# Gates of a delta-rule layer projected one round sooner and held in the buffers of y

## The chip, the cores and the metric

The kernel runs on one core of one Trainium2 chip. The core has five engines with a queue of instructions each: TensorE (PE, the matrix multiplier; its weight loads are listed as PEld), VectorE (DVE), ScalarE (ACT), GpSimd (POOL) and SyncE (SP, which here only starts transfers). The metric is device microseconds of one execution of the whole program. Three runs of the kernel before gave 2085.65, 2086.14 and 2088.14 us, median 2086.14.

## The reference

Two residual layers over 512 tokens of width 2048, float32. Layer 0 is gated differential attention, and this change doesn't touch it. Layer 1 is gated RWKV-7 time mixing, with 32 heads of 64 channels:

```
x = x + rwkv7_mixer(rms_norm(x), ...)

def rwkv7_mixer(h, ...):
    p = h @ w_in
    p = p + (token_shift(p) - p) * mu              # mix with the token before
    r, k, v, g, dw, da = split(p)
    decay, a = f(tanh(dw) @ decay_up), sigmoid(a0 + da @ iclr_up)
    kk = normalised(k * k_k);  k = k * (1 + (a - 1) * k_a)
    # S <- S*decay + (S @ -kk) (kk*a)^T + v k^T ;  y = S @ r     for each token, per head
    y = wkv7_scan(r, decay, k, v, -kk, kk * a)
    y = group_norm(y) * gn_w + gn_b + sum(r * k * r_k) * v
    return (y * silu(g)) @ w_out
```

## The kernel before

**Precision.** A float32 product is made of three TensorE products of operands split into a high and a low part (`mm3`, L118): 128 rows of weights, 512 tokens wide. Each weight tile is loaded by SP, its high part is cast by ACT (L109) and its low part subtracted by DVE (L110).

**Rounds.** Layer 1 (`layer1`, L1674) works on pairs of heads, 128 channels at a time, in sixteen rounds j = 0 to 15. A projection (`proj(i, j)`, `unit_chan`) of r, k, v or g for one pair is 16 k-steps of three matmuls, 48 in all; its result lies in one of two banks of PSUM until ACT and DVE mix it with the token before (`shift_mix`, L1173, lines L1177 and L1178). A round j issues in order: the values of pair j (`stage_v`), the keys of pair j + 1 (`begin`), from round 2 on the gate of pair j - 2 (`gate`, then `gated`), and the receptance of pair j + 1 (`receptances`). Round 1 has thus three projections, rounds 2 to 14 four, round 15 two. The gates of pairs 14 and 15 are projected after the last round, and then the output projection follows.

**The chunked scan.** The delta rule runs over eight chunks of 64 tokens. For pair j, `gram` makes the chunks' Gram matrices behind a matmul of the values' projection; `t_solve` (L1438 on) inverts their triangular 32 x 32 blocks in 31 dependent steps of two DVE operations (L1459, L1462), and turns the result (L1467, L1472); `t_first` and `t_second` (L1493, L1508) put the inverse of the 64 x 64 blocks together with small matmuls; `mask_gram` masks on POOL (L1411, L1413). One round later `scan_pair` (L1574 on) goes through the chunks: per chunk a matmul with the state (L1585), copies by ACT (L1588), a matmul with the inverse (L1598), copies (L1600), and a matmul with the keys (L1607) whose result DVE adds to the state (L1611; L1614 in the first chunk). Then the outputs are normalised, `finish_y` (L1669, L1671) transposes them, scales them and adds them to y, which `stage_v` has begun (L1524), and `gated` multiplies y into the gate (L1552) and stores the product in `yd2` (L1555), from where the output projection reads it.

**What sets the order.** Each matmul of a projection counts as a tick (`tick`). The scan is a list of steps that are issued so many ticks apart: `chain(g, j - 1, pair, delay, gap, gap_s, others)` waits `delay` ticks, then `gap` ticks after the first and the second matmul of a chunk and `gap_s` after the third; `others` are pieces hung on a chunk's end (`finish_y` on chunk 5). The solve is issued likewise, every three or four ticks (in the last round two or three), after a first pause of ten ticks or six. Pieces can also be hung on the n-th matmul of a projection ("behind"): the Gram matrices on 18 of the values (12 in round 1); in the receptance of round j - 1, `t_first` on 12, `mask_gram` on 27, `t_second` on 33 for j from 3 on, and on 24, 45 and 42 for j = 2. `t_first` issues at once whatever steps of the solve are left. From this, from priorities and from modelled durations a planner writes a fixed order for each engine's queue before the program runs; on the chip an engine takes its queue strictly in that order, waiting where an operand isn't ready.

**Buffers.** y has four buffers (`tag="y"`), taken in turn. The gate is mixed in the one buffer that the values have too (`tag="v"`), is multiplied there and stored from there.

Of the kernel before, what the change touches and what calls it, by code (L numbers as in the profile page):

```python
# [13 lines left out]
F32 = mybir.dt.float32  # L14
# [9 lines left out]
P = 128  # L24
D = 2048
T = 512
# [501 lines left out]
class Seven:  # L528
# [70 lines left out]
    def behind(self, raw, h, i):  # L599

        if h + 1 < NH:
            landed = self.g.nc.gpsimd.tensor_copy(self.mark[:], raw[:, 0, 0:1])
            with self.g.tc.issue_after(landed.ins):
                self.prime(h + 1, True, GROUPS[i : i + 1])
        return raw
# [566 lines left out]
@urgent  # L1172
def shift_mix(g, ps, rows, mu, omu, tag, bufs=2):  # L1173

    nc, w = g.nc, g.work
    o_ = w.tile([P, T], F32, name="mix" + tag, tag=tag, bufs=bufs)
    nc.scalar.activation(o_[:rows, :], ps[:rows, :], AF.Copy, scale=omu)  # L1177
    nc.vector.scalar_tensor_tensor(o_[:rows, 1:], ps[:rows, 0 : T - 1], mu, o_[:rows, 1:], ALU.mult, ALU.add)  # L1178
    return o_
# [77 lines left out]
LAG = 2  # L1257
# [11 lines left out]
def sum_channels(g, out, ones, x):  # L1269

    h, l = x
    g.nc.tensor.matmul(out, ones, h[:], start=True, stop=False)
    g.nc.tensor.matmul(out, ones, l[:], start=False, stop=True)
# [164 lines left out]
def t_solve(g, j, p):  # L1438


    nc, w = g.nc, g.work
    NQ = HALF // NG
    yield 3
    LT = g.low.tile([P, HALF, HALF], F32, name="LT", tag="LT", bufs=1)
    lt = nc.vector.transpose(LT[:].rearrange("p (r c) t -> p t r c", r=NG),
                        p.LP[:].rearrange("p c t -> p t c")[:, :, None, :].to_broadcast([P, HALF, NG, NC_]))
    Tm = w.tile([P, NQ, HALF], F32, name="Tm", tag="Tm", bufs=1)
    tmp = w.tile([P, NQ * HALF], F32, name="tmpl", tag="tmpl", bufs=1)
    nc.gpsimd.tensor_copy(Tm[:], g.unit[:])
    n2 = p.n2  # L1450
    behind(g, lt)
    with g.tc.issue_after(lt.ins):
        nc.vector.tensor_scalar(n2[:], n2[:], 1e-24, None, ALU.max)
        nc.vector.reciprocal(n2[:], n2[:])
    yield 10 if j >= LAG else 6
    for i in range(HALF - 1):
        n, s = HALF - 1 - i, i // NG + 1
        tt = tmp[:, : n * s].rearrange("p (a b) -> p a b", a=s)
        st = nc.vector.scalar_tensor_tensor(tt, LT[:, i : i + 1, i + 1 :].to_broadcast([P, s, n]), n2[:, i : i + 1],  # L1459
                                       Tm[:, 0:s, i : i + 1].to_broadcast([P, s, n]), ALU.mult, ALU.mult)  # L1460
        behind(g, st)
        nc.vector.tensor_add(Tm[:, 0:s, i + 1 :], Tm[:, 0:s, i + 1 :], tt)  # L1462
        yield (3 if j + 1 < D // P else 2) + i % 2
    nc.vector.tensor_mul(Tm[:], Tm[:], n2[:, None, :].to_broadcast([P, NQ, HALF]))
    p.T1 = w.tile([P, NC_, HALF], F32, name="T1", tag="T1", bufs=1)
    yield 9
    tt = nc.vector.transpose(p.T1[:].rearrange("p c (q r) -> p q r c", r=NG),  # L1467
                        Tm[:].rearrange("p q (r c) -> p q r c", r=NG))
    p.W = w.tile([P, NC_, HALF], F32, name="W", tag="Tm", bufs=1)
    behind(g, tt)  # L1470
    yield 4
    tt = nc.vector.transpose(p.W[:], p.T1[:])  # L1472
    behind(g, tt)
    for h in range(2):
        for half in range(2):
            o = half * HALF
            q = slice(h * C + o, h * C + o + HALF)
            nc.gpsimd.tensor_copy(g.TT[j % 2][q, :, h, o : o + HALF], p.W[q])
# [38 lines left out]
def stage_v(g, j, p, vps):  # L1517
    nc, w = g.nc, g.work
    col = lambda n: g.prm[n][:, j : j + 1]
    ps = g.ps.tile([P, 512], F32, name="pt", tag="pd", bufs=1)  # L1520
    sum_channels(g, ps[:], g.ones[:], split_act(g, p.rf[:], w, "x"))
    v = shift_mix(g, vps, P, *mus(g, 2, j), "v", 1)
    p.y = w.tile([P, T], F32, name="y", tag="y", bufs=4)
    nc.vector.tensor_mul(p.y[:], ps[:], v[:])  # L1524
    nc.scalar.activation(p.y[:], p.y[:], AF.Identity, bias=col("hgb"))
    p.v = v
# [15 lines left out]
def gate(g, j, gps, tag="v"):  # L1542
    nc, w = g.nc, g.work
    gt = shift_mix(g, gps, P, *mus(g, 3, j), tag, 1)
    th = w.tile([P, T], F32, name="thg", tag="thg", bufs=1)
    nc.scalar.activation(th[:], gt[:], AF.Tanh, scale=0.5)
    nc.vector.scalar_tensor_tensor(gt[:], th[:], 1.0, gt[:], ALU.add, ALU.mult)
    return gt


def gated(g, j, p, gt, last=False):
    g.nc.vector.tensor_mul(gt[:], gt[:], p.y[:])  # L1552
    if last:
        return
    g.nc.scalar.dma_start(out=g.yd2[j * P : (j + 1) * P, :], in_=gt[:])  # L1555
# [118 lines left out]
def layer1(g, aps):  # L1674
    nc, tc = g.nc, g.tc
    with ExitStack() as cx:
        g.lc = cx.enter_context(tc.tile_pool(name="lc1", bufs=1))
        g.work = cx.enter_context(tc.tile_pool(name="work1", bufs=2))
        rwkv_masks(g)
        w = g.work  # L1680
        pairs = []

        def proj(i, j, **k):
            return unit_chan(g, aps["rw_w_in"][i, j], P, **k)[0]
# [26 lines left out]
        for j in range(D // P):  # L1711
            p = pairs[j]
            if j:
                others = [(1, lambda p=p: turn_keys(g, p, 0)), (2, lambda p=p: turn_keys(g, p, 4)),
                          (4, lambda p=p: turn_values(g, p))]
                if j > 1:
                    others.append((5, lambda i=j - 2: finish_y(g, i, pairs[i])))
                full = LAG <= j < D // P - 1
                gaps = (7, 8) if full else (5, 6) if j > 1 else (4, 5)
                chain(g, j - 1, pairs[j - 1], 3 if j > 1 else 22, *gaps, others)  # L1720
            stage2(g, j, r, p)

            def behind(m, j=j, p=p):
                if j > 1:
                    pairs[j - 2].chain.finish(g)
                with tc.issue_after(m.ins):
                    gram(g, j, p)
                p.solve = Solve(g, t_solve(g, j, p))
            hooks = [(12 if 0 < j < LAG else 18, behind)]
            if j + 1 == D // P:  # L1730
                hooks.append((39, lambda m, p=p: [mask_gram(g, p, h, m) for h in range(2)]))
            stage_v(g, j, p, proj(2, j, behind=hooks))
            turns = ()
            if j == 0:
                turns = ((9, lambda m: turn_keys(g, p, 0)), (15, lambda m: turn_keys(g, p, 4)),
                         (27, lambda m: turn_values(g, p)))
            if j + 1 < D // P:
                begin(j + 1, turns)
            if j >= LAG:
                gated(g, j - LAG, pairs[j - LAG], gate(g, j - LAG, proj(3, j - LAG)))  # L1740
            if j + 1 < D // P:
                r = receptances(j + 1)
        chain(g, j, p, 3, 4, 5, whole=True)
        gps = proj(3, j - 1)
# [132 lines left out]
```

## Time and profile before

| | us |
|---|---|
| median of three runs | 2086.14 |
| profiled execution, its own time | 2087.84 |
| its span, first to last instruction | 2086.1 |
| layer 1's rounds, from the first receptance's end to the last one's | 977.5 to 1843.3 |
| round 1, round 2 | 53.2, 63.5 |
| each of rounds 3 to 13 | 59.1 to 59.2 |
| round 14 | 59.0 |

The profile is one execution; times are counted from its first instruction. PE is 99% busy, DVE 80%, ACT 60%, POOL 19%. A busy PE isn't a PE at its peak, since matmuls overlap in the array and their ends are modelled: what matters is the time from one matmul's start to the next, and the waits. Lines of groups read: line, engine, operation, out<-in, shapes, count | busy us, mean ns | idle time of the engine before them and what ended it. In a list of waits stand the total, the count and the longest. A round is counted here from the evacuation of one receptance (`mixr`, L1177 on ACT) to that of the next.

### The profile page before, as it was taken

What the parts mean: (1) busy time and instruction counts of PE and PEld (TensorE: products, weight loads), DVE (VectorE), ACT (ScalarE), POOL (GpSimd) and SP (SyncE); (2) the same over time, 40 slices, a digit from 0 to 9 for tenths busy, and PEclk for the clock granted to TensorE, in tenths of its full rate; (3) what the DMA queues carried; (4) which work ended last, traced back from release to release, by engine and by line L of the source; (5) the groups of instructions that cost most, each with busy time, mean ns of one, the idle gap of its engine ahead of it and who ended that gap; (6) DMA issues with size and microseconds to landing.
All of it is one profiled execution on the core that took longest, in us unless ns stands there. A gap on an engine that the chain in (4) does not pass through costs nothing.

```text
span 2086.1 us, 35354 instructions
## 1 busy us (share of the span) xinstructions
PE 2067.0 (99%) x12008; PEld 1708.6 (82%) x12008; DVE 1664.8 (80%) x4353; ACT 1250.9 (60%) x3005; POOL 406.2 (19%) x716
## 2 busy tenths in 40 slices
PE   9999999999999999999999999999999999999999
PEld 8888888888888888888778888888888888877887
DVE  5978778787877886576888888888888888887745
ACT  5766665666666664455666666666666666655333
POOL 0111011111111000101233332233333332342001
PEclk9999999999999999999999999999999999999999
DMA  6576777777777766742212222222222222235665
GB/s 200 146 181 178 182 187 190 181 193 180 190 175 192 182 222 196 169 118 93 79 64 79 80 78 69 82 79 82 76 79 79 79 79 74 89 126 166 204 163 120
DMA packets 101782, 280.71 MB, mean 135 GB/s; under 512 B 12545, under 2 KB 29073, under 8 KB 101601
## 3 DMA queue, kind: packets, MB, share of 16 engines
q1 hardware_dynamic: 68064, 198.90, 29.1%
q0 software_dynamic: 19104, 63.55, 16.4%
q10 hardware_dynamic: 14432, 16.01, 2.2%
q8 instruction: 94, 1.54, 0.3%
q14 instruction: 88, 0.71, 0.1%
HBM read 262.42 MB, written 15.99 MB: 133 GB/s over the span
## 4 chain that ended last, share of the span: by engine, by line
PE 92%; DVE 5%; ACT 2%; issue 1%; DMA 0%; POOL 0%; ACTq 0%; DVEq 0%; POOLq 0%
PE pp L118 70%; PE pt L118 6%; PE gp L1366 1%; PE sc L118 1%; PE sm L1585 1%; PE o L118 1%; PE sm L1607 1%; PE lora L118 1%; PE sm L1598 1%; PE z L118 1%; PE Y L1631 1%; DVE wl L110 1%; PE pt L359 1%; PE pt L1426 1%; PE px L1493 0%
## 5 line engine op out<-in xcount | busy, mean ns | idle before, releaser
L118 PE MATMUL pp<-hH,wh 128*128 128x512 f32 x1024 | 416.9, 407 | 0.0
L118 PE MATMUL pp<-hL,wh 128*128 128x512 f32 x1024 | 412.5, 403 | 0.0
L118 PE MATMUL pp<-hH,wl 128*128 128x512 f32 x1024 | 412.0, 402 | 0.0
L109 ACT CAST wh<-wraw 128x512 fp32r<-128x512 f32 (+1 forms) x412 | 253.8, 617 | 200.5 <-PE pp L118 103.5
L110 DVE TENSOR_TENSOR wl<-wraw,wh 128x512 fp32r<-128x512 f32 (+1 forms) x412 | 286.3, 696 | 102.6 <-ACT wh L109 98.7
L118 PE MATMUL pp<-wh,hH 128*128 128x512 f32 x932 | 366.5, 393 | 0.0
L118 PE MATMUL pp<-wh,hL 128*128 128x512 f32 x932 | 366.5, 393 | 0.0
L118 PE MATMUL pp<-wl,hH 128*128 128x512 f32 x932 | 364.4, 391 | 0.0
L118 PEld LDWEIGHTS pp<-hH,wh 128*128 128x128 f32 x1024 | 192.9, 188 | 37.6 <-issue 1.8
L118 PEld LDWEIGHTS pp<-hH,wl 128*128 128x128 f32 x1024 | 193.2, 189 | 32.8
L118 PEld LDWEIGHTS pp<-hL,wh 128*128 128x128 f32 x1024 | 193.3, 189 | 31.2
L118 PEld LDWEIGHTS pp<-wh,hL 128*128 128x128 f32 x932 | 175.1, 188 | 35.9
L118 PEld LDWEIGHTS pp<-wl,hH 128*128 128x128 f32 x932 | 175.2, 188 | 35.3 <-DVE wl L620 0.2
L118 PEld LDWEIGHTS pp<-wh,hH 128*128 128x128 f32 x932 | 175.3, 188 | 34.2
L620 DVE TENSOR_TENSOR wl<-wraw,wh 128x512 fp32r<-128x512 f32 x224 | 152.4, 688 | 60.0 <-ACT wh L619 59.4
L619 ACT CAST wh<-wraw 128x512 fp32r<-128x512 f32 x224 | 138.2, 620 | 93.8 <-PE pp L118 66.6
L1593 POOL COPY SA<-VS 64x64 f32<-64x64 f32 x224 | 75.1, 335 | 522.8 <-DVE VS L1611 466.4
L118 PE MATMUL pp<-wh,S 128*128 128x512 f32 x504 | 162.1, 395 | 0.0
L1459 DVE SCALAR_TENSOR_TENSOR tmpl<-LT,n,Tm 128x60 f32<-128x60 f32 (+24 forms) x496 | 135.6, 273 | 13.3
L582 POOL DMA_DIRECT2D T<-in_da_w_in_dram x63 | 53.7, 857 | 327.8 <-DVE wl L620 314.5
L1462 DVE TENSOR_TENSOR Tm<-Tm,tmpl 128x60 f32<-128x60 f32 (+24 forms) x496 | 106.2, 214 | 13.6
L619 ACT CAST wh<-T 128x512 fp32r<-128x512 f32 x126 | 77.8, 618 | 52.3 <-PE pp L118 52.2
(373 smaller groups left out, 3973.2 us busy)
## 6 DMA issues: line engine op xcount, KB each, us to landing
wraw<-in_rw_w_in_dram SPq DMA_DIRECT2D x128, 512.0 KB, 3.4
wraw<-in_da_w_in_dram SPq DMA_DIRECT2D x127, 512.0 KB, 4.3
T<-in_da_w_in_dram POOLq DMA_DIRECT2D x63, 512.0 KB, 6.1
wraw<-in_da_w_out_dram SPq DMA_DIRECT2D x26, 512.0 KB, 4.4
wraw<-in_rw_w_out_dram SPq DMA_DIRECT2D x26, 512.0 KB, 3.9
T<-in_da_w_in_dram SPq DMA_DIRECT2D x21, 512.0 KB, 4.3
wraw<-in_da_w_in_dram POOLq DMA_DIRECT2D x21, 512.0 KB, 6.9
yr<-yd SPq DMA_DIRECT2D x20, 256.0 KB, 3.1
```

Of the source, the lines that this page charges most:

```text
L109: nc.scalar.copy(hi[:], raw[:, k : k + n])
L110: g.split = nc.vector.tensor_sub(lo[:], raw[:, k : k + n], hi[:].bitcast(F32)).ins
L118: m = nc.tensor.matmul(out, a, b, start=s, stop=e, skip_group_check=skip)
L359: nc.tensor.transpose(pt[:, c * P : (c + 1) * P], t1s[t][:, c * P : (c + 1) * P], g.ident[:])
L582: self.g.nc.gpsimd.dma_start(out=raw, in_=src, accum_op=ALU.add)
L619: g.nc.scalar.copy(hi[:], raw[:, k])
L620: g.nc.vector.tensor_sub(lo[:], raw[:, k], hi[:].bitcast(F32))
L1366: m = nc.tensor.matmul(gp[h][:, i * P : (i + 1) * P], BK[r_, c0 + i, :, :], p.AR[r_, c0 + i, :, :], start=True, stop=True)
L1426: nc.tensor.transpose(ps[:, i * P : (i + 1) * P], p.BK[:, c0 + i].rearrange("p s t -> p (s t)"), g.ident[:])
L1459: st = nc.vector.scalar_tensor_tensor(tt, LT[:, i : i + 1, i + 1 :].to_broadcast([P, s, n]), n2[:, i : i + 1], Tm[:, 0:s, i : i + 1].to_br ...
L1462: nc.vector.tensor_add(Tm[:, 0:s, i + 1 :], Tm[:, 0:s, i + 1 :], tt)
L1593: nc.gpsimd.tensor_copy(p.SA[r_, c - 1, :], VS[r_, c, h, :])
```

## The change

One gate projection moves from round 14 to round 1. Rounds 1 to 13 project the gate of pair j - 1 and hold it, unmultiplied, for a round; round 14 projects none; round 15 projects that of pair 13, as before. The gate of pair j - 2, held since the round before, is multiplied with y and stored at matmul 36 of the next gate's projection (in round 14 after the keys' projection, in round 15 after the gate).

y and the held gates share four buffers that are allocated once and handed round in a list (`g.ys`). `shift_mix` with no tag takes the next of the list; after the product, the buffer of the gate goes back to the list first and the one of y behind it, so that in rounds 2 to 13 the new gate is mixed in the buffer whose product has just been sent to be stored.

The scan's gaps change with the work of the rounds: (6, 7) in round 1 instead of (4, 5), (5, 6) in rounds 14 and 15 (round 14 had (7, 8)), (7, 8) in the others. The solve's first pause is ten ticks from round 1 on (it was six in rounds 0 and 1). The matmuls on which `t_first`, `mask_gram` and `t_second` hang stay as they are.

```diff
@@ shift_mix
-    o_ = w.tile([P, T], F32, name="mix" + tag, tag=tag, bufs=bufs)
+    o_ = w.tile([P, T], F32, name="mix" + tag, tag=tag, bufs=bufs) if tag else g.ys.pop(0)
@@ t_solve
-    yield 10 if j >= LAG else 6
+    yield 10 if j else 6
@@ stage_v
-    p.y = w.tile([P, T], F32, name="y", tag="y", bufs=4)
+    p.y = g.ys.pop(0)
@@ layer1
+        g.ys = [w.tile([P, T], F32, name="y", tag="y", bufs=4) for _ in range(4)]
...
-                full = LAG <= j < D // P - 1
-                gaps = (7, 8) if full else (5, 6) if j > 1 else (4, 5)
+                gaps = (6, 7) if j == 1 else (7, 8) if j < D // P - 2 else (5, 6)
                 chain(g, j - 1, pairs[j - 1], 3 if j > 1 else 22, *gaps, others)
...
                 begin(j + 1, turns)
-            if j >= LAG:
-                gated(g, j - LAG, pairs[j - LAG], gate(g, j - LAG, proj(3, j - LAG)))
+            def finished(m, i=j - LAG):
+                with tc.issue_after(m.ins):
+                    gated(g, i, pairs[i], held)
+                g.ys.extend((held, pairs[i].y))
+
+            if j == D // P - 2:
+                finished(g.m)
+            elif j:
+                last = j == D // P - 1
+                gps = proj(3, j - 1 - last, behind=[(36, finished)] if j >= LAG and not last else ())
+                held = gate(g, j - 1 - last, gps, None)
+                if last:
+                    finished(g.m)
             if j + 1 < D // P:
                 r = receptances(j + 1)
```

## The prediction

> **What bounds the kernel now.** I read the page first, then the second layer cut at the ends of its rounds, then what TensorE (PE) waits for there. From the page:
>
> ```profile
> span 2086.1 us, 35354 instructions
> PE 2067.0 (99%) x12008; PEld 1708.6 (82%) x12008; DVE 1664.8 (80%) x4353; ACT 1250.9 (60%) x3005; POOL 406.2 (19%) x716
> PE 92%; DVE 5%; ACT 2%; issue 1%; DMA 0%; POOL 0%; ACTq 0%; DVEq 0%; POOLq 0%
> ```
>
> PE carries 92% of the chain that ends last, so a change is worth the PE time it removes or inserts. A round ends with the receptance, whose evacuation is the mark (first in round 0, last at the end of round 14):
>
> ```profile
> L1177 ACT ACTIVATE mixr<-pp,omu x16: 672/674/692, 977.5 to 1843.3; 128x512 f32<-128x512 f32 x16
> ```
>
> Busy time by stretch, columns PE, PEld, DVE, ACT, POOL, PEclk, DMA share, GB/s:
>
> ```profile
> 1016.80:1070.00 53.20, 50.30 (x433) 39.84 (x432) 44.18 (x124) 36.64 (x93) 17.68 (x37) 1.00 0.19 63
> 1070.00:1133.50 63.50, 62.12 (x423) 51.01 (x422) 55.07 (x143) 38.41 (x97) 22.56 (x40) 0.97 0.24 81
> 1192.70:1251.80 59.10, 59.10 (x421) 49.02 (x421) 52.46 (x139) 37.71 (x95) 18.03 (x35) 1.00 0.23 79
> 1784.30:1843.30 59.00, 59.00 (x421) 48.91 (x421) 52.18 (x143) 37.53 (x94) 19.04 (x36) 1.00 0.33 104
> 1016.80:1133.50 116.70, 112.43 (x854) 90.85 (x853) 99.24 (x266) 75.05 (x189) 40.24 (x76) 0.99 0.22 73
> 1784.30:1893.60 109.30, 106.44 (x753) 86.37 (x752) 94.77 (x262) 64.23 (x167) 34.17 (x68) 1.00 0.36 115
> 1070.00:1076.00 6.00, 4.91 (x24) 3.50 (x22) 5.75 (x11) 2.73 (x8) 5.88 (x8) 1.00 0.53 179
> 1076.00:1088.00 12.00, 11.71 (x69) 10.02 (x70) 8.79 (x23) 7.30 (x22) 1.37 (x5) 0.86 0.12 44
> ```
>
> Round 1 (three projections) and round 2 (four) come first, then a steady round and round 14, each with four. A steady round has no idle PE. PE's waits in rounds 1 and 2, then from round 15 to 1910 us:
>
> ```profile
> PE sm L1585 <- DVE VS L1614: 1.5, 1, 1.5
> PE px L1493 <- DVE T L1467: 0.8, 2, 0.4
> PE sm L1585 <- POOL G L1411: 0.8, 1, 0.8
> PE sm L1598 <- ACT rhs L1588: 0.8, 2, 0.5
> PE sm L1607 <- ACT VS L1600: 0.3, 1, 0.3
> ```
> ```profile
> PE sm L1585 <- DVE VS L1611: 1.7, 2, 0.9
> PE sm L1607 <- ACT VS L1600: 1.0, 2, 0.7
> ```
>
> So the rounds with little projection work are where the scan, the 32-step solve and VectorE (DVE) show through.
>
> **The change, part by part.** PE does the same work; one gate projection moves from round 14 to round 1. Twelve of its matmuls, from start to start:
>
> ```profile
> 999.65 0.39 PE L118 MATMUL pp<-hL,wh 128*128 128x512 f32 x1
> ...
> 1002.37 0.39 PE L118 MATMUL pp<-hL,wh 128*128 128x512 f32 x1
> ```
>
> 2.72 / 12 = 0.227 us, times 48 is 10.9 us.
>
> *Rounds 1 and 2.* Round 1 becomes a steady one plus the 64 small matmuls of pair 0's inverse that slipped into it. 32 of those took 0.69 us; the four of a finish, which round 1 doesn't have, cover about 0.5:
>
> ```profile
> L1669 PE MATMUL pt<-ident,yc x4: 273/273/273, 1230.7 to 1231.0; 128*128 128x128 f32 x4
> ```
> ```profile
> 1066.33 0.69 PE L1493 MATMUL px<-T,G 32*32 32x32 f32 x32 [0.45 <-DVE T L1467]
> ```
>
> (64 - 4 are the 433 less 421 - 48 instructions of the rows above.) So 59.1 + 1.4 - 0.5 = 60.0, and with round 2 119.1 against today's 116.7. That is +2.4 for 10.9 us of work, 8.5 us gained, if nothing waits. Of the 8.5, 4.2 us are the five waits, 1.7 us the clock (12 us at 0.86), the rest delays too short for a row. Not all goes: round 2 still masks its Gram blocks at matmul 45 of the receptance, so the waits on POOL and on the following copy (0.8 + 0.8) can return; the first wait was DVE taking solve steps ahead of the first state, which a wider gap eases. Left over: 0 to 2.4, I take 1.4, nearest to those two rows.
>
> *Rounds 14 and 15.* Round 14 goes from 59.0 to 48.1 us of PE work. The groups of DVE that the gate leaves, in a steady round (four of the sixteen weight splits, the gate's own 0.65, one of two evacuations), then the solve's products in a steady round:
>
> ```profile
> L110 DVE TENSOR_TENSOR wl<-wraw,wh 128x512 fp32r<-128x512 f32 x16 | 11.3, 704 | 1.3 <-ACT wh L109 1.2
> L1547 DVE SCALAR_TENSOR_TENSOR mixv<-thg,mixv 128x512 f32<-128x512 f32 x1 | 0.7, 650 | 0.0
> L1178 DVE SCALAR_TENSOR_TENSOR mixv<-pp,prmin_rw_mu_dram,mixv 128x511 f32<-128x511 f32 x2 | 1.4, 714 | 0.1
> ```
> ```profile
> L1459 DVE SCALAR_TENSOR_TENSOR tmpl<-LT,n,Tm x31: 226/273/318, 1203.7 to 1235.7; 128x60 f32<-128x60 f32 x3, 128x28 f32<-128x28 f32 x2, 128x54 f32<-128x54 f32 x2, 128x48 f32<-128x48 f32 x2
> ```
>
> DVE sheds 4 x 0.70 + 0.65 + 0.71 = 4.2 us and keeps the product of gate 12. So round 14 needs 48.0 us of DVE in 48.1 of PE, where round 1, which waited, had 44.2 in 53.2. The solve is paced by matmuls (31 steps, 108 of them). It starts 31 in, and the receptance asks for the inverse at its matmul 12, which is now 96 + 12 = 108 instead of 156: 22 steps are done, nine are forced. Round 1 asked at 120 with three left, and PE waited up to 0.45 us at that place.
>
> Price by DVE's share: from 1784.3 to 1893.6 us it needs 94.8 - 4.2 = 90.6 us. PE would take 109.3 - 10.9 = 98.4. At a steady round's 88.8% the stretch is 102.1 us, a loss of 3.7; at this stretch's own 86.7%, 104.5, 6.1; at the 85.0% of rounds 1 and 2, 106.5, 8.1. The lower end is 2.7, what round 15 waits today with the same scan gaps (5, 6) and a denser solve. I take 5.0, between the first two, since late work may run on into the gate projections after the last round.
>
> *Steady rounds, 2 to 13.* Gate, product and store stay one each; the product comes 12 matmuls before the projection's end. The gate lands in the buffer whose product has just been stored:
>
> ```profile
> 1236.46 0.69 ACT L1177 ACTIVATE mixv<-pp,omu 128x512 f32<-128x512 f32 x1
> ...
> 1240.60 0.88 DVE L1552 TENSOR_TENSOR mixv<-mixv,y 128x512 f32<-128x512 f32 x1
> 1241.51 0.33 ACTq L1555 DMA_DIRECT2D yd<-mixv  x1
> ```
> ```profile
> DMA to landing us min/median/max: 2.0/2.0/3.4
> ```
>
> The product can start 12 x 0.227 = 2.7 us before the end; with 0.9 for it and 2.0 to 3.4 to landing the buffer is free 0.2 to 1.6 us after the end. ScalarE (ACT) then evacuates that late; behind it stand the scan's copies and the casts of the next weights. The scan's first matmul and its copies:
>
> ```profile
> L1588 ACT COPY rhs<-sm 64x64 f32<-64x64 f32 x256 | 52.4, 205 | 63.1 <-PE sm L1585 60.1
> L1585 PE MATMUL sm<-VS,G 128*128 128x128 f32 x256 | 50.0, 276 | 4.2 <-DVE VS L1611 1.7 <-DVE VS L1614 1.5 <-POOL G L1411 0.8
> ```
>
> A scan gap of seven matmuls is 7 x 59.1/192 = 2.2 us, of which a matmul and two copies take 0.7, so up to 1.5 us is covered. I take 0; below nothing is excluded since PE has no idle there.
>
> *At no cost:* the solve's longer first pause in round 1 (four matmuls, inside a round that is 10.9 us longer); SP's two weight loads that move with the gate, into a stretch whose DMA share is 0.19; POOL's queue, past which nothing moves; the tail, whose order is unchanged and which absorbs late pairs.
>
> Sum: -8.5 + 1.4 + 5.0 + 0 = -2.1 us on the profiled execution, whose own time was 2087.84, 1.7 above the median of 2086.14. Off the median: 2084.0 us. A measurement of this kernel tells about 0.2%, 4.2 us, from no change.
>
> [...] The clock fell to half for about 3.4 us (1.7 / 0.5) right after 1070 to 1076, where PE was busy 4.91 of 6 us and no wait exceeded 0.8. [...]
>
> **Rivals.** *Cheap round 14:* late work runs on, and only round 15's 2.7 us comes back, with nothing left in rounds 1 and 2: -8.5 + 2.7 = -5.8, 2080.3. For it: round 15 lives with these gaps. Against it: 48.0 us of DVE in 48.1.
>
> *The forced solve holds PE (slower).* Steps late in round 1's solve, each half behind another DVE operation, and one step in round 15 beside a POOL mask:
>
> ```profile
> 1059.38 0.22 DVE L1459 SCALAR_TENSOR_TENSOR tmpl<-LT,n,Tm 128x28 f32<-128x28 f32 x1
> ...
> 1063.71 0.22 DVE L1459 SCALAR_TENSOR_TENSOR tmpl<-LT,n,Tm 128x8 f32<-128x8 f32 x1
> ```
> ```profile
> 1856.38 1.16 POOL L1413 TENSOR_SCALAR_AFFINE_SELECT G<-G 64x1024 f32<-64x1024 f32 x1
> ```
> ```profile
> 1856.49 1.08 DVE L1459 SCALAR_TENSOR_TENSOR tmpl<-LT,n,Tm 128x29 f32<-128x29 f32 x1
> ```
>
> Three steps took 4.33 us, 1.44 each, against 0.49 of DVE's own time: nine forced ones take 13.0 instead of 4.4 us. If PE's order has the inverse's matmuls where 4.4 would put them, PE stands 8.6 us there: -2.1 + 8.6 = +6.5, 2092.6. It decides from a stand of 2.1 us, and is slower by over 0.2% from 6.3. Against it: in round 1 that order was off by 0.45 us only. [...]
>
> *The held buffer makes ACT late:* the 0.2 to 1.6 us stand in front of the copies and 0.5 of it reaches PE, in twelve rounds: +6.0, 2090.0. Against it: the 1.5 us of cover.
>
> **How the numbers follow.** Forecast 0.45 (own range 2080 to 2088), cheap round 14 0.22, forced solve 0.20, held buffer 0.13. Faster by over 0.2%: 0.14 of the forecast's and the cheap round's 0.22: 0.36. Slower: 0.15 of the forced solve, 0.10 of the held buffer, 0.02: 0.27. The same: 0.37. The range takes in the cheap round (2080.3, less its doubt) and most of the two slow ones: 2079.0 to 2092.0.
>
> **What would show it.** Rounds 1 and 2 together near 120.5 us with hardly a wait in round 1; round 14 at 51 to 53 instead of 48.1; DVE at 90% or more there; the steps of round 14's solve crowded after its matmul 108. Wrong, if rounds 3 to 13 leave 59.1 us, if PE waits over 3 us at L1493 in round 14, or if round 14 ends within a microsecond of 48.1.

## The result, and the profile after

The changed kernel takes 2096.22 us (median of five runs, 2093.22 to 2098.21) against 2086.14 before: a ratio of 1.0043, 95% interval 1.0032 to 1.0054. It is slower, by about twice what a measurement of this kernel can tell from no change. The forecast was 2084.0; even the upper end of the range, 2092.0, is below the fastest run. The profiled execution took 2096.19 us, 8.35 more than the profiled one of before.

From the page of the changed kernel, the span, the busy time and the chain that ended last:

```profile
span 2094.3 us, 35322 instructions
PE 2072.0 (99%) x12008; PEld 1709.9 (82%) x12008; DVE 1658.7 (79%) x4353; ACT 1256.4 (60%) x3005; POOL 393.7 (19%) x716
PE 89%; DVE 7%; ACT 2%; issue 1%; DMA 0%; POOL 0%; ACTq 0%; SPq 0%; DVEq 0%; POOLq 0%
```

The same 12008 matmuls, and PE's share of the last chain falls from 92% to 89% while VectorE's rises from 5% to 7%: PE waits for VectorE more than before. The marks at the rounds' ends, and busy time by stretch (columns PE, PEld, DVE, ACT, POOL, PEclk, DMA share, GB/s) for rounds 1 and 2, a steady round and round 14, then for two short stretches:

```profile
L1177 ACT ACTIVATE mixr<-pp,omu x16: 675/677/687, 977.1 to 1847.5; 128x512 f32<-128x512 f32 x16
```
```profile
1016.50:1079.40 62.90, 61.80 (x482) 49.33 (x481) 51.89 (x140) 40.90 (x102) 20.64 (x41) 1.00 0.23 78
1079.40:1143.50 64.10, 61.68 (x424) 50.95 (x424) 52.42 (x133) 38.23 (x94) 19.68 (x36) 0.97 0.23 72
1202.90:1262.30 59.40, 59.25 (x423) 49.05 (x422) 51.77 (x139) 38.23 (x95) 16.99 (x35) 1.00 0.25 78
1797.10:1847.50 50.40, 47.50 (x306) 38.21 (x305) 44.60 (x123) 30.16 (x80) 13.41 (x29) 1.00 0.31 97
1084.00:1092.00 8.00, 6.31 (x43) 5.44 (x44) 2.97 (x6) 3.65 (x14) 0.91 (x3) 0.79 0.13 47
1848.00:1852.00 4.00, 4.00 (x69) 2.90 (x64) 4.00 (x13) 2.16 (x5) 2.43 (x4) 0.57 0.24 75
```

From mark to mark, and beside it what the prediction's sum gave:

| stretch (us) | before | after | predicted | after less predicted |
|---|---|---|---|---|
| up to round 1 | 1016.8 | 1016.5 | 1016.8 | -0.3 |
| rounds 1 and 2 | 116.7 | 127.0 | 120.5 | +6.5 |
| rounds 3 to 13 | 650.8 | 653.6 | 650.8 | +2.8 |
| round 14 to the end | 301.8 | 297.2 | 295.9 | +1.3 |
| span | 2086.1 | 2094.3 | 2084.0 | +10.3 |

So 10.9 us of PE work left round 14, and only 4.6 us came back there; rounds 1 and 2, which were to take the work in for 3.8, took 10.3; and each of rounds 3 to 13 became 0.25 us longer (59.16 to 59.41).

PE's waits in rounds 1 and 2, in a steady round, and from round 14 to 1912 us:

```profile
PE sm L1598 <- ACT rhs L1588: 2.3, 1, 2.3
PE sm L1585 <- DVE VS L1614: 0.7, 1, 0.7
PE px L1493 <- DVE T L1467: 0.4, 1, 0.4
```
```profile
PE gp L1366 <- DVE AR L1351: 0.2, 1, 0.2
```
```profile
PE px L1493 <- DVE T L1467: 2.2, 1, 2.2
PE sm L1585 <- DVE VS L1611: 1.7, 2, 1.0
...
```

The five rows of waits in rounds 1 and 2, 4.2 us, did shrink to three, 3.4 us, but one of them is 2.3 us. The two waits of over 2 us are each followed by a stretch at half clock (0.50 from 1088 to 1090 us and from 1849 to 1851): 8 us at a mean of 0.79 and 4 us at 0.57 are 1.7 us of lost clock each.

*Where the 2.3 us at L1598 come from.* The timeline of the changed kernel at the turn from round 1 to round 2, first POOL, then VectorE, then ScalarE (start, duration, in square brackets the idle time ahead and what ended it):

```profile
1078.61 0.69 POOL L1411 TENSOR_SCALAR_AFFINE_SELECT G<-G 64x512 f32<-64x512 f32 x1
...
1080.47 1.20 POOL L1411 TENSOR_SCALAR_AFFINE_SELECT G<-G 64x512 f32<-64x512 f32 x1
1081.63 1.60 POOL L1413 TENSOR_SCALAR_AFFINE_SELECT G<-G 64x1024 f32<-64x1024 f32 x1
```
```profile
1077.58 0.17 DVE L70 SCALAR_TENSOR_TENSOR rs_i<-rs_t,rs_i 128x8 f32<-128x8 f32 x1
...
1078.32 2.11 DVE L70 SCALAR_TENSOR_TENSOR rsg<-rs_t,rs_i 128x8 f32<-128x8 f32 x1
...
1081.07 1.14 DVE L110 TENSOR_TENSOR wl<-wraw,wh 128x512 fp32r<-128x512 f32 x1
...
1083.81 0.75 DVE L1352 SCALAR_TENSOR_TENSOR mixr<-mixr,prm_hrk,f 128x512 f32<-128x512 f32 x1
```
```profile
1084.59 0.62 ACT L1145 CAST sHx<-mixr 128x512 fp32r<-128x512 f32 x1 [2.49 <-DVE mixr L1352]
1085.12 0.42 ACT L1588 COPY rhs<-sm 64x64 f32<-64x64 f32 x2
```

It is read from below. PE's L1598 needs the copies `rhs` (L1588), which stand in ScalarE's fixed order behind the cast L1145 and start at 1085.12, though the matmul that they copy from (L1585) started at 1082.19 and took 0.39; the cast idles 2.49 us for VectorE's L1352; VectorE is late because its operations stretch while POOL masks pair 1's Gram blocks: the 128x8 product took 2.11 us beside the first two masks and 0.17 us just before them, the split L110 1.14 where its mean was 0.70 before. The masks hang on matmul 45 of 48 of the receptance that ends round 1, so they fall on the first work of round 2. That is still only an argument from a trace; the first two experiments test it.

The kernel before has the same chain at the same place, where round 1 ends at 1070.04: a mask, VectorE's 128x8 product beside it, and the cast that idles for L1352.

```profile
1071.69 1.67 POOL L1413 TENSOR_SCALAR_AFFINE_SELECT G<-G 64x1024 f32<-64x1024 f32 x1
```
```profile
1072.27 1.11 DVE L70 SCALAR_TENSOR_TENSOR rs_i<-rs_t,rs_i 128x8 f32<-128x8 f32 x1
```
```profile
1075.20 0.62 ACT L1145 CAST sHx<-mixr 128x512 fp32r<-128x512 f32 x1 [2.13 <-DVE mixr L1352]
```

There too `rhs` stands behind the cast, PE waits (0.5 us at L1598), and 1.7 us of clock are lost (12 us at 0.86). So by the traces round 2, 63.5 us before and 64.1 after, has not caught something new: it has kept a loss of over 4 us that the change didn't touch, since the masks stayed on matmul 45.

### The profile page after: what moved, and what is told of

It reads as the page before. It is cut to its first block, busy times and chain, and to the rows that moved or that the text cites. A ratio compares the mean times of both kernels' runs of the same rounds, so it can differ in the third digit from the quotient of the medians.

```text
span 2094.3 us, 35322 instructions
## 1 busy us (share of the span) xinstructions
PE 2072.0 (99%) x12008; PEld 1709.9 (82%) x12008; DVE 1658.7 (79%) x4353; ACT 1256.4 (60%) x3005; POOL 393.7 (19%) x716
## 4 chain that ended last, share of the span: by engine, by line
PE 89%; DVE 7%; ACT 2%; issue 1%; DMA 0%; POOL 0%; ACTq 0%; SPq 0%; DVEq 0%; POOLq 0%
PE pp L118 67%; PE pt L118 6%; DVE wl L110 2%; PE gp L1366 2%; PE sc L118 1%; PE o L118 1%; PE sm L1585 1%; PE lora L118 1%; PE sm L1607 1%; PE sm L1598 1%; PE z L118 1%; PE Y L1631 1%; PE pt L359 1%; PE pt L1426 1%; PE px L1493 0%
## 5 line engine op out<-in xcount | busy, mean ns | idle before, releaser
L109 ACT CAST wh<-wraw 128x512 fp32r<-128x512 f32 (+1 forms) x412 | 254.2, 618 | 224.4 <-PE pp L118 128.2
L110 DVE TENSOR_TENSOR wl<-wraw,wh 128x512 fp32r<-128x512 f32 (+1 forms) x412 | 292.0, 710 | 99.4 <-ACT wh L109 94.6
L118 PEld LDWEIGHTS pp<-hH,wh 128*128 128x128 f32 x1024 | 193.1, 189 | 37.7 <-issue 2.3
L620 DVE TENSOR_TENSOR wl<-wraw,wh 128x512 fp32r<-128x512 f32 x224 | 152.6, 688 | 59.1 <-ACT wh L619 58.5
L1462 DVE TENSOR_TENSOR Tm<-Tm,tmpl 128x60 f32<-128x60 f32 (+24 forms) x496 | 106.5, 215 | 13.1
```

Of the source, the lines that this page charges most:

```text
L109: nc.scalar.copy(hi[:], raw[:, k : k + n])
L110: g.split = nc.vector.tensor_sub(lo[:], raw[:, k : k + n], hi[:].bitcast(F32)).ins
L118: m = nc.tensor.matmul(out, a, b, start=s, stop=e, skip_group_check=skip)
L620: g.nc.vector.tensor_sub(lo[:], raw[:, k], hi[:].bitcast(F32))
```

## The experiments

Each is the changed kernel with the edit shown, unless said otherwise. The kernel before was run beside them: medians of 2086.0 to 2087.2 us. Round lengths are from mark to mark in the profiled execution. A hook is the matmul on which a piece of work is hung.

**The hooks of round 1 at the steady rounds' matmuls.**

```diff
-                behind += [(27 if j > 2 else 45, lambda m: [mask_gram(g, pairs[j - 1], h, m) for h in range(2)]),
-                           ({1: 18, 2: 24}.get(j, 12), piece(t_first, j - 1, pairs[j - 1])),
-                           ({1: 39, 2: 42}.get(j, 33), piece(t_second, j - 1, pairs[j - 1]))]
+                behind += [(45 if j == 1 else 27, lambda m: [mask_gram(g, pairs[j - 1], h, m) for h in range(2)]),
+                           ({1: 18}.get(j, 12), piece(t_first, j - 1, pairs[j - 1])),
+                           ({1: 39}.get(j, 33), piece(t_second, j - 1, pairs[j - 1]))]
```

> The changed kernel, but in the receptance of round 1 the inverse's two halves and the masking hang on matmuls 12, 33 and 27, as in every later round, instead of 24, 42 and 45. Theory (late masks): POOL then masks pair 1 inside round 1, so that VectorE is not held up at the turn to round 2; PE's wait of 2.3 us at L1598 and the half clock after it go, and round 2 falls from 64.1 us to below 60.5, 3.6 us or more off the time. Rival (backlog): VectorE is late there from the work itself; then a wait of 1 us or more remains at the start of round 2 and round 2 stays above 62.

2090.81 us, ratio 1.0018 (1.0008 to 1.0028): 5.4 below the changed kernel. Round 2 goes from 64.1 to 59.6 and the wait at L1598 is gone; round 1 stays at 62.8.

**Of these hooks the mask alone.**

```diff
-                behind += [(27 if j > 2 else 45, lambda m: [mask_gram(g, pairs[j - 1], h, m) for h in range(2)]),
+                behind += [(45 if j == 1 else 27, lambda m: [mask_gram(g, pairs[j - 1], h, m) for h in range(2)]),
```

> The changed kernel, with only the mask of pair 1 moved, from matmul 45 to matmul 27 of round 1's receptance; the two pieces of the table work stay at 24 and 42. With all three moved the time was 2090.81 us, 5.4 below the changed kernel. Theory 1: the POOL masks that run into round 2 and stretch VectorE's products are the whole cause, so this alone takes round 2 from 64.1 to 59.7 us or so and gives 2091 us. Theory 2: the table pieces on VectorE and ScalarE at 42 weigh too, since they stand in the same crowded stretch: round 2 stays at 61.5 to 63 and the time at 2093 to 2095 us.

2091.40 us (2090.03 to 2093.37), ratio 1.0022 (1.0013 to 1.0031). Its POOL in round 1, its PE's waits in rounds 1 and 2, and its round 2:

```profile
1071.80 0.65 POOL L1411 TENSOR_SCALAR_AFFINE_SELECT G<-G 64x512 f32<-64x512 f32 x1
...
1075.11 1.17 POOL L1413 TENSOR_SCALAR_AFFINE_SELECT G<-G 64x1024 f32<-64x1024 f32 x1
```
```profile
PE sm L1585 <- DVE VS L1614: 0.7, 1, 0.7
PE px L1493 <- DVE T L1467: 0.4, 1, 0.4
```
```profile
1080.40:1140.00 59.60, 59.60 (x425) 49.43 (x424) 50.41 (x133) 38.21 (x96) 16.13 (x33) 1.00 0.24 78
```

The masks are done 4 us before the round ends instead of 4 us behind it, PE's wait of 2.3 us and the half clock are gone, and round 2 is as short as with all three hooks moved. Of the three hooks the mask's is the whole of it: 4.6 us of round 2, 2.3 of them the wait and 1.7 the clock behind it.

**y's buffer ahead of the gate's.**

```diff
-                g.ys.extend((held, pairs[i].y))
+                g.ys.extend((pairs[i].y, held))
```

> The changed kernel, but the two buffers go back to the list in the other order, y's first: the new gate is mixed in y's buffer, whose last reader is the product on VectorE, and not in the one that is still being stored. Theory (held buffer): the 0.25 us that every round from 3 to 13 has gained come from the gate's evacuation waiting for the store; the gate is then evacuated some 2 us earlier in the round, the wait at L1366 goes, and those rounds return to 59.1 to 59.2 us, 2.8 us off the time. Rival (order): the 0.25 us come from the product's new place or from the planner's other order; the rounds stay at 59.4.

2092.65 us, ratio 1.0033 (1.0020 to 1.0046): 3.6 below. Rounds 3 to 13 are back at 59.16 us each, 2.8 in all, and PE has no wait in them. What this undoes can be seen in the changed kernel, where the gate lands in the buffer that has just been stored (from the instructions on the tile `y`, 1150 to 1300 us, first and last start of each group, and one line of what VectorE idled for, in two rounds; then the last matmul of the first of these gates):

```profile
L1552 DVE TENSOR_TENSOR y<-y x2: 683/684/684, 1186.6 to 1246.0; 128x512 f32<-128x512 f32 x2
L1555 ACTq DMA_DIRECT2D yd<-y x2: 326/326/327, 1187.3 to 1246.7; - x2
L1177 ACT ACTIVATE y<-pp,omu x2: 688/688/688, 1189.8 to 1249.2; 128x512 f32<-128x512 f32 x2
L1547 DVE SCALAR_TENSOR_TENSOR y<-thg,y x2: 1074/1078/1082, 1194.2 to 1253.7; 128x512 f32<-128x512 f32 x2
...
  ACT thg L1546: 3.3, 2
...
DMA to landing us min/median/max: 2.0/2.0/2.0
```
```profile
1186.62 0.39 PE L118 MATMUL pp<-hH,wl 128*128 128x512 f32 x1
```

The product, hung on matmul 36, is reached by VectorE only when the last matmul starts. The evacuation of the gate starts 2.5 us after the store is issued and 2.8 us after the projection's end at 1187.0, that is 13.1 us ahead of the round's end at 1202.9, where before it was 15.4 (1251.84 less 1236.46). ScalarE's L1546 on the gate is late by it, VectorE's L1547 idles 1.6 us a round for it (0.2 in this run), and VectorE stays behind: AR (L1351) starts 3.4 us after the round's end instead of 2.3, and PE waits up to 0.2 us at L1366. The order of ScalarE's queue differs between the two kernels too. In the changed kernel a weight cast (L109) that waits for PE until 1189.13 stands ahead of the evacuation; the store alone, landing 2.0 us after 1187.33, would have held it until 1189.3. How much is the store and how much the planned order round it is not separated; the product's place is the same in both, and so is not the cause. In this run's profiled execution the wait in round 14 was followed by a longer stretch at half clock, which took back 2.5 us:

```profile
1845.00:1856.00 11.00, 10.60 (x88) 8.06 (x90) 7.54 (x24) 6.20 (x16) 4.52 (x9) 0.53 0.29 90
```

**Both mends** (the three hooks and the buffers' order).

> The changed kernel with both mends: round 1's receptance pieces at 12, 27 and 33, and the product's buffer given out ahead of the gate's. Theory (two causes that add): 5.4 from the first and 2.8 from the second off 2096.2 make 2088.0 us, rounds 3 to 13 at 59.16 and round 2 at 59.6; what is then left above the time before is rounds 14 and 15. Rival (they overlap, since both act by VectorE being late in the receptance): 2089.5 to 2091 us. A half clock of 10 us after the wait in round 14, as seen once, would add some 3 us to either.

2088.94 us (2087.31 to 2091.12), ratio 1.0009 (1.0000 to 1.0019): 7.3 below the changed kernel, where 5.4 and the 2.8 us of the rounds make 8.2. Rounds 1, 2 and 3 to 13 are 62.8, 59.16 and 59.16; round 14 to the end is 297.3, as in the changed kernel. The two causes add in the rounds. What is left over the kernel before is too small for a measurement to tell.

**The narrow gaps back in round 1.**

```diff
-                gaps = (6, 7) if j == 1 else (7, 8) if j < D // P - 2 else (5, 6)
+                gaps = (4, 5) if j == 1 else (7, 8) if j < D // P - 2 else (5, 6)
```

> The changed kernel with the narrow scan gaps (4, 5) back in round 1, as before the change. Theory 1: the wider gaps (6, 7) are what keeps the first states from catching VectorE and ScalarE late; without them waits of 1 to 2 us come back at the scan's lines in round 1, and the time is 2097.5 to 2099 us. Theory 2: the added projection itself gives VectorE the room and the gaps do nothing: round 1 is within 0.5 us of 62.9 and the time 2095.5 to 2097 us. A gap that only moved the scan's end later would show a shorter round 1 and round 2 here, 2094 us or less.

2094.77 us (2094.04 to 2095.59), ratio 1.0038 (1.0024 to 1.0052); rounds 1 and 2 are 63.1 and 63.5, 0.4 less together than the changed kernel's. The wider scan brought nothing that can be measured: the first state's wait at L1585, 1.5 us before, is 0.7 with either gaps, and the narrow ones add two waits of 0.3 to 0.4 in round 1. So it is not the gaps that eased the first wait; whether it was the added projection or the solve's longer first pause, which the change brought with it, no run separates. The time came out 0.7 below theory 2's band, whose round 1 fits.

**Round 14's hooks later.** The receptance that ends round 14 asks for the solve at matmul 24, masks at 45 and does the second part at 42.

```diff
-                behind += [(27 if j > 2 else 45, lambda m: [mask_gram(g, pairs[j - 1], h, m) for h in range(2)]),
-                           ({1: 18, 2: 24}.get(j, 12), piece(t_first, j - 1, pairs[j - 1])),
-                           ({1: 39, 2: 42}.get(j, 33), piece(t_second, j - 1, pairs[j - 1]))]
+                behind += [(45 if j < 3 or j == D // P - 1 else 27, lambda m: [mask_gram(g, pairs[j - 1], h, m) for h in range(2)]),
+                           ({1: 18, 2: 24, 15: 24}.get(j, 12), piece(t_first, j - 1, pairs[j - 1])),
+                           ({1: 39, 2: 42, 15: 42}.get(j, 33), piece(t_second, j - 1, pairs[j - 1]))]
```

> The changed kernel, but in the receptance of round 14, which now has three projections, the inverse hangs on matmul 24, the masking on 45 and the second half on 42, as in round 1. Theory (forced solve): fewer steps of the solve are forced and none runs beside a mask; PE's wait of 2.2 us at L1493 goes below 1 us, round 14 with what follows gains 2 to 4 us. Rival (backlog passed on): VectorE is full in this round wherever the hooks stand; the masks then meet the start of round 15 as they meet that of round 2, a wait of 1 to 2.5 us appears at L1585 or L1598 there, and the time is within 1.5 us of the changed kernel's.

2095.30 us, ratio 1.0046 (1.0029 to 1.0063). Round 14 is 0.9 us shorter, but PE still waits 2.2 us at L1493 and the rest is as long as in the changed kernel. This is the rival's time, but the wait that it expected at the start of round 15 didn't come (0.5 us at most in front of a state's matmuls there): the wait at L1493 stayed.

**Pair 14's solve at a faster pace** (a step every two or three matmuls in place of three or four).

```diff
-        yield (3 if j + 1 < D // P else 2) + i % 2
+        yield (3 if j + 2 < D // P else 2) + i % 2
```

> The changed kernel, but the solve of round 14 takes a step every two or three matmuls, as that of round 15 does, so that its 31 steps are done by the 108 matmuls at which the inverse is asked for. Theory (forced solve): the wait at L1493 goes, 2 to 4 us off the time. Rival (VectorE full): the denser steps delay the scan's states in the first two projections; new waits of 1 to 3 us at L1585 there, no gain.

2095.47 us, ratio 1.0044 (1.0029 to 1.0059). The wait at the solve shrinks to 1.2 us and another takes its place, for another VectorE result:

```profile
PE pt L1273 <- DVE sLx L1146: 3.0, 1, 3.0
```

Round 14 takes 55.0 instead of 50.4 us and the rest 243.0 instead of 246.8. In these two orders of round 14's work nothing is gained, which fits a VectorE that is short of time: it is 44.6 of 50.4 us busy with a solve in its midst, some of whose steps stand beside the masks. From the changed kernel's round 14, POOL and VectorE:

```profile
1835.57 1.15 POOL L1413 TENSOR_SCALAR_AFFINE_SELECT G<-G 64x1024 f32<-64x1024 f32 x1
```
```profile
1835.00 0.65 DVE L1459 SCALAR_TENSOR_TENSOR tmpl<-LT,n,Tm 128x42 f32<-128x42 f32 x1
1835.58 2.22 DVE L1308 TENSOR_TENSOR_SCAN l<-rmask,th 128x512 f32<-128x512 bf16 x1
1837.72 0.58 DVE L1462 TENSOR_TENSOR Tm<-Tm,tmpl 128x42 f32<-128x42 f32 x1
...
1838.33 1.11 DVE L1459 SCALAR_TENSOR_TENSOR tmpl<-LT,n,Tm 128x35 f32<-128x35 f32 x1
```

The three operations on `tmpl` and `Tm` here, two halves of one step and the first of the next, stretch over 4.4 us, where the median of such a product is 0.27 us; the scan between them takes 2.2.

**The round without a gate moved on to round 15.** This run and all that follow hold both mends. Rounds 1 to 14 project a gate; round 15 projects none; the gates of pairs 14 and 15 follow the loop, as before. From the edit, shortened:

```diff
-                gaps = (6, 7) if j == 1 else (7, 8) if j < D // P - 2 else (5, 6)
+                gaps = (6, 7) if j == 1 else (7, 8) if j < D // P - 1 else (5, 6)
...
-            if j == D // P - 2:
+            if j == D // P - 1:
                 finished(g.m)
...
-        gts.append(gate(g, j, proj(3, j, behind=[(24, last_but_one)]), "E"))
+        gts.append(gate(g, j, proj(3, j, behind=[(42, last_but_one)]), "E"))
```

> Both mends, and the round without a gate projection is round 15 in place of round 14: rounds 1 to 14 project a gate with gaps (7, 8), round 15 projects value, key and decay for the last time but no gate, and the two left-over gates follow the loop. Theory 1: rounds 14 and 15 lost 6.3 us because round 14 needs 48 us of VectorE in 48 us of TensorE with a solve to force; round 15 has no next receptance and no next solve in the loop, so the same cover is missed less: round 14 stays at 59.2, the wait at the solve's matmul is gone from it, and the time is 2081 to 2084 us. Theory 2 (the missing cover costs the same wherever it is taken out): the waits turn up in round 15 and behind it, and the time is 2087 to 2089 us.

2081.69 us (2080.41 to 2082.74), ratio 0.9976 (0.9966 to 0.9986). Here, and in the next two runs, pair 13's product is formed before that pair's normalised output has been added to y, so that this row of the result is another one; the amount of work is the same.

**The same with pair 13's product behind the loop**, at matmul 36 of the first gate projection.

> Both mends, the round without a gate projection is round 15 in place of round 14, and the product of pair 13 stands at matmul 36 of the first of the two gate projections behind the loop, so that pair 13 is finished ahead of it; nothing else is left out. Theory 1 (the cover is missed less where no solve has to be forced): rounds 2 to 14 all at 59.2, no long wait at the solve's matmul, and what is left over the stretch after round 14 under 2 us: 2081 to 2084 us, faster than the kernel before by 0.2 to 0.3%. Theory 2 (VectorE's backlog only moves behind the loop): waits of 2 us and more at the scan's lines or at the output weights after round 15, and 2086 to 2089 us.

2081.54 us, ratio 0.9976 (0.9966 to 0.9986). Round 14 is 59.3 and the wait at L1493, 2.8 us with both mends, is 0.4; round 14 to the end takes 290.6 us, against 301.8 less the 10.9 us of a projection, 290.9: nothing is lost there any more.

**The same with pair 0's scan four matmuls later** in round 1 (`3 if j > 1 else 26`).

> The same kernel with pair 0's scan started four matmuls later in round 1 (a delay of 26 in place of 22). Theory 1: the first state's wait of 0.7 us and the 0.4 us ahead of it are VectorE taking solve steps first, so a later start removes them: round 1 goes from 62.8 to 61.8 and the time down by 0.7 to 1 us. Theory 2: VectorE is simply full there, the wait moves with the scan and its end comes later: round 1 within 0.3 us of 62.8, the time within 1 us of the other run.

2079.49 us (2078.61 to 2081.10), ratio 0.9967 (0.9955 to 0.9980). Round 1 goes from 62.9 to 62.1 us and the first state's wait from 0.8 to 0.4, nearly as theory 1 has it; of the 2.4 us between the two profiled executions another 1.3 lie ahead of round 0's mark, where the two kernels are the same.

**Pair 13's product behind its finish**, at matmul 18 of the last gate projection; the edit is against the run before.

```diff
-        gts = [gate(g, j - 1, proj(3, j - 1, behind=[(36, finished)]))]
+        gts = [gate(g, j - 1, proj(3, j - 1))]
...
-        gts.append(gate(g, j, proj(3, j, behind=[(42, last_but_one)]), "E"))
+        gts.append(gate(g, j, proj(3, j, behind=[(18, finished), (42, last_but_one)]), "E"))
```

> The kernel with the mends, with round 15 as the one without a gate projection and with pair 0's scan at a delay of 26, and now with pair 13's product put at matmul 18 of the last gate projection, behind that pair's finish, which the scan reaches 93 matmuls after round 15 has begun (in the three runs with the product at matmul 48 or 84 it was formed from the unfinished pair). Nothing is left out. Theory 1: the product is 0.9 us of VectorE and a store, with 30 more matmuls of cover behind it, so the time stays at 2079 to 2081.5 us, 0.2 to 0.35% below the kernel before. Theory 2: the later store of row 13 makes the output projection wait for its reload: PE waits over 0.5 us at the output weights and 2082 to 2085 us.

2085.47 us (2082.75 to 2087.23), ratio 0.9990 (0.9981 to 0.9999): 6.0 above the run before. Between the two profiled executions it is 6.4, of which 2.1 lie ahead of round 0's mark, where the kernels are the same, and 4.4 from round 14 to the end. Neither theory foresaw the place. PE's longest wait from round 15 to 1912 us, and ScalarE at that place in the run before and in this one:

```profile
PE px L1508 <- ACT X L1496: 3.2, 1, 3.2
```
```profile
1893.66 0.74 ACT L1496 COPY X<-px 32x256 f32<-32x256 f32 x2 [0.34 <-PE px L1493]
...
1896.25 0.62 ACT L474 CAST hH<-yr 128x512 fp32r<-128x512 f32 x1
```
```profile
1900.19 0.62 ACT L474 CAST hH<-yr 128x512 fp32r<-128x512 f32 x1 [1.29 <-DMA yr<-yd]
...
1901.35 0.74 ACT L1496 COPY X<-px 32x256 f32<-32x256 f32 x2
```

In the run before, the inverse's copies for pair 15 (L1496) stand ahead of ScalarE's last three casts (L474) of reloaded rows of y (`yr`); here they stand behind them, and two of these casts wait 3.9 us for their reloads. The reloads are not issued later: the last six begin 37.7 us after round 14's end in the run before (1884.00 less 1846.33) and 37.8 here (1885.95 less 1848.20), and the last of them is issued 7 us after the product's store has landed; it takes 7.4 us to land, where the one in the run before took 5.7. So it is not theory 2, a reload that waits for the later store. The product's new place changed ScalarE's planned order, which put casts that wait for reloads ahead of copies that PE waits for, and the last reload took longer; what each is worth is not separated here.

**With a delay of 30** instead of 26.

> The same with pair 0's scan another four matmuls later (30). From 22 to 26 round 1 went from 62.9 to 62.1 us and the first state's wait from 0.8 to 0.4. Theory 1: the rest of that wait goes too, round 1 61.7 and the time 0.4 us lower. Theory 2: the scan's end now runs into the next pair's table work and the 0.4 us is given back: round 1 and 2 together the same within 0.3 us.

2085.21 us, ratio 0.9994 (0.9985 to 1.0003): no difference to the run above. Round 1 is 61.9 against 62.0, and rounds 1 and 2 together are the same, as theory 2 has it.

**Pair 13's finish earlier instead of its product later.** In round 15 the finish hangs on the scan's fourth state, the product stands at matmul 36 of the first gate projection, the delay is 26.

```diff
-                    others.append((5, lambda i=j - 2: finish_y(g, i, pairs[i])))
+                    others.append((5 if j < D // P - 1 else 3, lambda i=j - 2: finish_y(g, i, pairs[i])))
```

> Both mends, delay 26, round 15 as the one without a gate projection, pair 13's product back at matmul 36 of the first gate projection behind the loop, and pair 13's finish hung on the scan's fourth state instead of its sixth in round 15, 61 matmuls after the round has begun, so that it stands ahead of the product; nothing is left out. Theory 1 (the place of the product behind the loop cost the 6 us, by making the last reloads late that ScalarE's queue stands on): no wait at the inverse's second part, 2079 to 2082 us, 0.2 to 0.35% below the kernel before. Theory 2 (forming the product from a finished pair costs it wherever it stands, since VectorE is full there): a wait of 2 us or more in front of the second part, and 2084 to 2086 us.

2080.82 us (median of 11, 2079.38 to 2083.54), ratio 0.9974 (0.9965 to 0.9983), with nothing left out: 5.9 us below the kernel before on the same chip. Rounds 1 and 2 take 62.0 and 59.2 us. PE's longest waits from round 15 to 1912 us:

```profile
PE sm L1585 <- DVE VS L1611: 1.2, 2, 0.9
PE px L1508 <- ACT X L1496: 1.1, 1, 1.1
PE pt L1669 <- ACT TT L1511: 0.6, 1, 0.6
```

The 3.2 us in front of the inverse's second part are 1.1 here. Theory 1 had none, but its time holds. Its reason, the late reload, holds in part: the last reload is issued 43.8 us after round 14's end in place of 44.5 and takes 6.1 us to land in place of 7.4, 2.0 us earlier in all. But the copies still stand behind the casts in ScalarE's order, and 1.1 us of the wait is left. Round 14 to the end is 291.5 us: 0.6 over the 290.9 that would lose nothing, where the changed kernel lost 6.3.

No run moves the mask or the scan's start in the kernel before, which had the masks' loss too. How much of the 5.9 us they would give there without the gate's move is open.

## Why the prediction was wrong, step by step

*Rounds 1 and 2: the step that failed.* What failed is the term "left over: 0 to 2.4, I take 1.4". Against the base of 119.1 us (60.0 and 59.1) it measured 7.9: 5.0 in round 2 and 2.9 in round 1. The prediction counted round 2's 63.5 less 59.1 us, its waits and its half clock, among the 8.5 that a fuller round 1 would bring back. It named the cause (round 2 "still masks its Gram blocks at matmul 45 of the receptance"), but priced it by two waits of PE, 0.8 + 0.8, and took part of that. What the masks cost is more: they stretch VectorE (2.11 us for a product of 0.17), VectorE holds ScalarE's cast (2.49 us), the cast holds the scan's copies (PE waits 2.3 us for them), and half clock follows (1.7 us). The change left them where they were and the loss stayed, in a slightly larger size: 4.6 us of round 2, shown by moving the mask alone. Some 0.4 more of round 2 is the buffers' order (59.5 to 59.16). The 2.9 of round 1 are 1.1 of waits at L1585 and L1493 and delays too short for a row; the wider gaps, to which the prediction gave the easing of the first wait, did nothing, and a later start of the scan took 0.8 off. With the mends and that later start the two rounds take 121.2 us, 2.1 above the base and within the range of 0 to 2.4: the base can nearly be reached, but not with the masks where the change left them.

*Steady rounds: a zero that was 0.25 us, eleven times.* The sign that the prediction set for this (rounds 3 to 13 leave 59.1) came true. Two steps of the working failed. The product was to start 2.7 us before the projection's end, so that the buffer would be free 0.2 to 1.6 us after it; VectorE reached it only as the last matmul started, and the evacuation began 2.8 us after the end. And the harm was looked for at the scan's copies, where 1.5 us of cover were found; it came by the gate's own chain, ScalarE's L1546 and VectorE's L1547, into VectorE's work for the receptance, and out at the Gram matmuls (L1366). The size, 2.8 us, is shown by the order of two names. The rival "held buffer" had the cause at 0.5 us a round and was given 0.13.

*Rounds 14 and 15: near, 6.3 for 5.0.* Round 14 took 50.4 (51 to 53 was forecast), VectorE's share there is 44.6 / 50.4 = 88%, just under the 90% named, and the rest of the loss runs on to the end, as the choice of 5.0 assumed. The bounds of 2.7 and 8.1 held. The rival "forced solve" had the place, L1493, and the masks beside the solve's steps (one product took 1.08 us beside a mask in the kernel before, one 1.11 in the changed kernel, where the median is 0.27), but its price of 8.6 us was far off: 2.2 and, in this execution, 1.7 of clock. That VectorE's time is what lacks there, rather than its order, is argued and not shown: the two runs that reordered round 14 without gain fit it, and so does the last one, which took the gate from round 15 instead and lost only 0.6 us, but that run also moved other work.

*The clock.* The sum has no half clock in round 14. The profiled execution paid it there once, 1.7 us (4 us at 0.57, behind the wait of 2.2 us); round 2 still pays it too (8 us at 0.79), which the prediction had counted among its gains.

*The scale.* Each of the three sized terms was too favourable: 6.5, 2.8 and 1.3 us. The range took in one of the slow rivals at a time, never two.

## What to carry to other kernels

Before a delay is counted among the gains of a change, find the piece of work that causes it and ask whether the change moves that piece. Work that is moved into a round meets hooks that were placed for that round as it was; ask of each (here the masks, beside which a product of 0.17 us took 2.11) what it runs beside, and price the whole chain of delays that it starts, not only the wait in which PE shows it. In a chain of queues that run in a fixed order, as ScalarE's here, where copies stood behind a cast that idled 2.49 us, follow a delay through every engine that shares the result, not only to the nearest consumer. Where a stretch must lose its cover, take it from the one with the least of the pacing side engine's work: here the stretch from round 14 to the end went from 297.3 to 291.5 us when the same projection was left out one round later, with the product and the finish of one pair placed anew.

## What the runs showed of the hardware that was not expected

PE's clock fell to half (0.50 from 1088 to 1090 us in the changed kernel) after waits of 2 to 3 us, but not each time, and in the kernel before (0.50 from 1078 to 1080) after a crowded stretch with no wait above 0.8. With both mends and with the mask alone PE had the same wait of 2.8 us at L1493 in round 14; the stretches at its end and behind it, first with both mends, then with the mask alone:

```profile
1839.00:1845.00 6.00, 4.91 (x74) 3.68 (x75) 6.00 (x16) 3.85 (x9) 2.79 (x5) 0.72 0.40 127
```
```profile
1843.80:1849.00 5.20, 4.82 (x80) 3.60 (x81) 5.20 (x14) 4.48 (x12) 3.33 (x5) 1.00 0.39 130
```

One lost 0.28 x 6 = 1.7 us, the other nothing; in the run with y's buffer first, behind a wait of 2.2 us, it was 0.47 x 11 = 5.2. These are one, none and three times 1.7, so by estimate half clock lasted one or three times 3.4 us (1.7 / 0.5). Why the same wait halved the clock in one run and not in the other is not shown. None of the waits that were seen in front of a half clock in layer 1 was longer than 3.2 us (at L1508 in the run with pair 13's product behind its finish, where the clock was 0.92 from 1898 to 1904 us and 0.79 from 1904 to 1910).

A single VectorE product of 128x8 took twelve times its own time (2.11 us for 0.17, changed kernel, at 1078.32) beside two GpSimd masks.
